# Two key heads and two chunks at once: pairing half-array matmuls in the attention and in the recurrent chain

## The chip, the cores and the metric

The kernel runs on one core of a Trainium2 chip. Its time is the device time of one launch in microseconds (us). Five engines run side by side, each through its own list of instructions in order: PE (TensorE, matmuls), DVE (VectorE), ACT (ScalarE), POOL (GpSimd) and SP (SyncE, which issues transfers here). PE multiplies a stationary operand, which it loads first, by a moving one that streams through.

## What is computed

A model block of 512 tokens by 1024 features in float32, and then two hybrid layers. Each hybrid layer runs three mixers on the same normed input (sliding-window attention, a gated recurrence, a retention), sums them under gates, and ends with a feed-forward part. The change touches two of the mixers. Cut to what matters:

```python
def sliding_window_attention(q, k, v, sinks):      # 8 query heads, 2 key heads of 64, blocks of 128
    s = einsum('bnqhgd,bnshd->bnhgqs', qb, kb) * 64 ** -0.5      # h: key head, g: its 4 query heads
    s = where(mask, s, -inf)                                     # a band of 128 keys back
    m = maximum(max(s), sink);  p = exp(s - m)
    p = p / (sum(p) + exp(sink - m))
    o = einsum('bnhgqs,bnshd->bnqhgd', p, vb)

def rwkv7_time_mix(...):                           # 8 heads of 64
    def step(S, (r, w, k, v, a, b)):
        Sa = S @ a
        S = S * w + outer(Sa, b) + outer(v, k)
        return S, S @ r                            # y: the outputs
```

## The kernel before, in words

Activations lie with features on the partitions, 512 tokens along the free axis. Dense products are done tile by tile (`dense`, `mac`): one M tile is 8 k tiles, each in three passes (lines 135 to 137) of a 128x128 weight against 512 tokens, 24 passes in all. The weight's two parts come from a cast on ACT (line 125, `whi`) and a subtraction on DVE (line 126, `wlo`); both have two buffers.

Dense tiles that nobody waits for yet stand in a queue, each with a cost of 5.2 or 5.6. The mixers call `pump(us)` between their own steps: it adds to a credit and starts as many queued tiles as the credit pays. `attention` pumps `pa` = 7.0 per block and key head, the chain `pc` = 2.5 per chunk. In the end a list scheduler at build time sets the order of instructions on every engine; the order is fixed before the launch.

**The chain** (`rwkv_chain`) goes through 8 chunks of 64 tokens in each layer. For chunk c, line 1001 adds what the state S[c] gives to `pr`, DVE copies it (line 1003), line 1012 multiplies it by the chunk's inverse, ACT copies the result into `UV` (line 1014), line 1020 makes the update of the state, POOL decays the old state (line 1026) and DVE adds the update in two halves (line 1030). `ahead(c+1)` (lines 970 and 976) prepares the next chunk apart from the state. The states stand in three buffers in turn (named srst, wd and wa in the trace). `outputs` makes a chunk's outputs: for each of 4 pairs of heads one product with the state (line 986, moving side 128 wide) and two with the values (line 989, 64 wide). The chunk's outputs go to 64 of the 128 PSUM partitions, the lower half for even chunks, the upper for odd ones, so they use one half of the array's columns. ACT copies them out (line 991).

**The attention** goes through 4 blocks of 128 queries. The key heads are in the two halves of the partitions: head 0 in rows 0 to 63 of `q` and `k`, head 1 in rows 64 to 127. For each block and each key head j in turn: scores of 4 query heads (line 1169, 64 rows of the array, 256 keys or, in the first block, 128), times scale and plus mask on DVE (line 1173), the row maximum (line 1175), exp on ACT (line 1184), division by the sum (line 1188), transposes on PE for each 128 keys (line 1192), a copy (line 1194), and the product with the values (line 1195: 64 columns of the array, moving side 512 wide) into the half of `po` that belongs to j. The score tiles `as` have two buffers.

A float32 product is done as two passes in the trace (so one instruction of the program stands as x2); a transpose and a float32r pass stand once.

## Time and profile before

| | |
|---|---|
| median of three timed runs | 2668.3 us (2667.89 to 2669.66) |
| profiled execution, first to last instruction (span) | 2666.0 us |
| what lies around the span, by the median | 2.3 us |
| PE busy | 2579.1 us, 97% of the span |
| DVE / ACT / POOL busy | 56% / 34% / 14% |
| one layer's chain (first layer) | about 860 to 941 us |
| one layer's attention (first layer) | about 1015 to 1125 us |

No time of its own is given for the profiled execution beside its span; the timed runs lie 1.9 to 3.7 us above the span. The second layer repeats chain and attention at about 1866 to 1941 us and 2020 to 2140 us. A row of the timeline begins with its start and the time from the first start to the last end of the merged instructions; ends of matmuls are modelled and overlap the next start, so what a group takes on PE is read from one row's start to the next row's start.

### The profile page before, as it was taken

Reading aid. Unit: us, or ns where it says so; the run is one execution under the profiler, and the core shown is the slowest. Engines: PE = TensorE matmul, PEld = TensorE weight load, DVE = VectorE, ACT = ScalarE, POOL = GpSimd, SP = SyncE. Lnnn points to the kernel's source line nnn. Section 1 sums busy time; section 2 is a strip of 40 time slices with the busy share of each in tenths; the row PEclk is TensorE's granted clock in tenths of the full one; section 3 lists DMA queues with packets and bytes.
Section 4 is the critical chain, followed back from the end, with each engine's and each line's share of the span. In section 5 each row is a group of like instructions: output and inputs, shape, how many; then the busy total and the mean of one; then the engine's idle time right before and its main releaser. Section 6 shows DMA issues by size and latency. Waiting matters only on the chain. (4 is left out here: it accounts for less than half of the span.)

```text
span 2666.0 us, 33302 instructions
## 1 busy us (share of the span) xinstructions
PE 2579.1 (97%) x13104; PEld 2052.8 (77%) x13104; DVE 1491.5 (56%) x2546; ACT 893.7 (34%) x1342; POOL 378.5 (14%) x277
## 2 busy tenths in 40 slices
PE   8989999999998999999999999998999999999999
PEld 6767888887776877677788887767877677788887
DVE  8775666336788455565443333788455565444322
ACT  4343444225332333522322222322333423332221
POOL 2111111013120001005311101120000004211100
PEclk9999999999999999999999999999999999999999
DMA  4132223334223143226422334223152226422332
GB/s 148 64 103 85 98 95 95 93 104 139 87 91 107 60 154 95 70 87 206 137 95 97 99 123 127 83 80 107 43 174 88 79 72 213 143 95 95 99 114 96
DMA packets 99502, 282.51 MB, mean 106 GB/s; under 512 B 13201, under 2 KB 14225, under 8 KB 99217
## 3 DMA queue, kind: packets, MB, share of 16 engines
q1 hardware_dynamic: 97616, 277.52, 31.8%
q10 hardware_dynamic: 1728, 2.87, 0.3%
q8 instruction: 103, 1.69, 0.3%
q14 instruction: 55, 0.44, 0.1%
HBM read 244.42 MB, written 31.72 MB: 104 GB/s over the span
## 5 line engine op out<-in xcount | busy, mean ns | idle before, releaser
L125 ACT CAST whi<-wraw 128x1024 fp32r<-128x1024 f32 (+1 forms) x400 | 414.6, 1037 | 1110.1 <-PE mm L136 735.1
L126 DVE TENSOR_TENSOR wlo<-wraw,whi 128x1024 fp32r<-128x1024 f32 (+1 forms) x400 | 491.9, 1230 | 246.6 <-ACT whi L125 237.1
L1352 POOL TENSOR_TENSOR fg<-fg,rb 128x512 f32<-128x512 f32 x44 | 78.3, 1780 | 396.1 <-ACT fg L1351 396.1
L135 PE MATMUL mm<-x0h,whi 128*128 128x512 f32 x286 | 116.2, 407 | 8.1 <-ACT x0h L165 8.1
L220 POOL TENSOR_TENSOR acc<-acc,sq 128x512 f32<-128x512 f32 x49 | 77.8, 1587 | 325.9 <-ACT sq L219 325.9
L137 PE MATMUL mm<-x0h,wlo 128*128 128x512 f32 x286 | 114.1, 399 | 6.0 <-DVE wlo L126 5.7
L135 PE MATMUL mm<-x2h,whi 128*128 128x512 f32 x286 | 114.3, 400 | 2.2 <-ACT x2h L165 2.2
L136 PE MATMUL mm<-x0l,whi 128*128 128x512 f32 x286 | 113.7, 397 | 1.2 <-DVE x0l L169 1.2
L136 PE MATMUL mm<-x2l,whi 128*128 128x512 f32 x286 | 114.6, 401 | 0.0
L136 PE MATMUL mm<-x5l,whi 128*128 128x512 f32 x286 | 112.9, 395 | 1.6 <-DVE x5l L169 1.6
L135 PE MATMUL mm<-x3h,whi 128*128 128x512 f32 x286 | 113.9, 398 | 0.0
L137 PE MATMUL mm<-x1h,wlo 128*128 128x512 f32 x286 | 113.7, 398 | 0.0
L136 PE MATMUL mm<-x3l,whi 128*128 128x512 f32 x286 | 113.1, 395 | 0.7 <-DVE x3l L169 0.7
L137 PE MATMUL mm<-x2h,wlo 128*128 128x512 f32 x286 | 113.7, 398 | 0.0
L136 PE MATMUL mm<-x1l,whi 128*128 128x512 f32 x286 | 113.3, 396 | 0.3 <-DVE x1l L169 0.3
L1354 DVE TENSOR_TENSOR fg<-fg,mm 128x512 f32<-128x512 f32 x44 | 30.3, 688 | 148.8 <-PE mm L137 148.8
L135 PE MATMUL mm<-x5h,whi 128*128 128x512 f32 x286 | 113.4, 397 | 0.0
L137 PE MATMUL mm<-x6h,wlo 128*128 128x512 f32 x286 | 113.3, 396 | 0.0
L135 PE MATMUL mm<-x6h,whi 128*128 128x512 f32 x286 | 113.3, 396 | 0.0
L135 PE MATMUL mm<-x7h,whi 128*128 128x512 f32 x286 | 113.2, 396 | 0.0
L137 PE MATMUL mm<-x7h,wlo 128*128 128x512 f32 x286 | 113.1, 396 | 0.0
L135 PE MATMUL mm<-x1h,whi 128*128 128x512 f32 x286 | 113.1, 395 | 0.0
(757 smaller groups left out, 6132.5 us busy)
## 6 DMA issues: line engine op xcount, KB each, us to landing
wraw<-in_w_in_dram SPq DMA_DIRECT2D x138, 512.0 KB, 3.5
wraw<-in_w_ffn_dram SPq DMA_DIRECT2D x88, 512.0 KB, 3.4
wraw<-in_w_up_dram SPq DMA_DIRECT2D x44, 512.0 KB, 3.3
wraw<-in_w_ffn_down_dram SPq DMA_DIRECT2D x32, 448.0 KB, 3.4
wraw<-in_w_out_dram SPq DMA_DIRECT2D x24, 512.0 KB, 3.5
gates<-gt SPq DMA_DIRECT2D x48, 256.0 KB, 2.1
cg<-gates SPq DMA_DIRECT2D x32, 256.0 KB, 3.8
gt<-xres SPq DMA_DIRECT2D x32, 256.0 KB, 3.3
```

What stands on the lines that cost most here:

```text
L125: nc.scalar.copy(hi[:, :n], raw[:, :n])
L126: nc.vector.tensor_tensor(lo[:, :n], raw[:, :n], hi[:, :n].bitcast(F32), ALU.subtract)
L135: self.nc.tensor.matmul(ps, hi[:, c], xh, start=first and k == 0, stop=False)
L136: self.nc.tensor.matmul(ps, hi[:, c], xl, start=False, stop=False)
L137: self.nc.tensor.matmul(ps, lo[:, c], xh, start=False, stop=last and k == n - 1)
L220: (eng or nc.gpsimd).tensor_tensor(acc, acc, s, ALU.add)
L1352: nc.gpsimd.tensor_tensor(g, g, rb, ALU.mult)
L1354: nc.vector.tensor_tensor(g, g, ps, ALU.mult)
```

## The change

In the chain, `outputs` is called only after every second chunk and makes the outputs of chunks c and c+1 together: for each step one product for the even chunk into partitions 0 to 63 and one for the odd chunk into 64 to 127, in turn. One ACT copy of 128 partitions takes the place of two of 64. `ahead(c + 1)` is written before the inverse's product rather than behind it. In the attention, the scores of both key heads are written in turn (row halves 0 and 1), both heads' softmaxes follow, then for each 128 keys both heads' transposes and copies, and then the two products with the values, one behind the other. `pump` is called once more for each 128 keys: 7.0 in the first block, 3.5 twice in the others, so that a layer's attention pays 84 of credit rather than 56. Otherwise the diff takes out comments and docstrings.

```diff
         def outputs(c, S, Y):
             py = self.tile(self.mm, [P, 512], "mm")
-            yo = slice(64 * (c % 2), 64 * (c % 2) + 64)
-            uv = UV[c % 2][:, c // 2]
             for p in range(4):
-                if S is not None:
-                    nc.tensor.matmul(py[yo, p * P:(p + 1) * P], AR[:, p, c, CH:], S[:, p], start=True, stop=False)
+                for e in range(2):
+                    if S[e] is not None:
+                        nc.tensor.matmul(py[64 * e:64 * e + 64, p * P:(p + 1) * P], AR[:, p, c + e, CH:], S[e][:, p],
+                                         start=True, stop=False)
                 for j in range(2):
                     h = 2 * p + j
-                    nc.tensor.matmul(py[yo, h * 64:h * 64 + 64], SC[:, h, c, CH:], uv[:, h * 64:h * 64 + 64],
-                                     start=S is None, stop=S is None or j == 1)
-            nc.scalar.copy(Y[yo], py[yo])
+                    for e in range(2):
+                        nc.tensor.matmul(py[64 * e:64 * e + 64, h * 64:h * 64 + 64], SC[:, h, c + e, CH:],
+                                         UV[e][:, c // 2, h * 64:h * 64 + 64], start=S[e] is None,
+                                         stop=S[e] is None or j == 1)
+            nc.scalar.copy(Y, py)
...
@@ -1001,10 +1004,11 @@
                         nc.tensor.matmul(pr[bh, p * P:(p + 1) * P], AR[:, p, c, 0:CH], S[c][:, p], start=False, stop=p == 3)
                 R = self.tmp(self.tb)
                 nc.vector.tensor_copy(R[bh], pr[bh])
-            if c:
-                if c % 2:
-                    Ys.append(self.tmp(self.tb))
-                outputs(c - 1, S[c - 1], Ys[-1])
+                if c < NCH - 1:
+                    nx = ahead(c + 1)
+            if c and c % 2 == 0:
+                Ys.append(self.tmp(self.tb))
+                outputs(c - 2, S[c - 2:c], Ys[-1])
             if c == NCH:
                 break
             pu = self.psum()
@@ -1013,7 +1017,6 @@
                                  start=True, stop=True)
             nc.scalar.copy(uv[bh], pu[bh])
             if c < NCH - 1:
-                nx = ahead(c + 1)
                 pS = self.psum()
                 for h in range(8):
                     o = slice(64 * (h % 2), 64 * (h % 2) + 64)
...
@@ -1157,22 +1160,23 @@
         ol = self.tile(op, [P, 4, T], "o1", F32R)
         for b in range(NW):
             k0 = 0 if b else P
-            nk = 256 - k0
-            po = self.psum()
-            for j in range(2):
-                o = slice(64 * j, 64 * j + 64)
-                s = self.tile(ap, [P, 4, 256], "as", bufs=2)
-                mx = self.small("am", 4)
-                for u in range(2):
-                    ps = self.psum()
-                    for i in range(2):
-                        nc.tensor.matmul(ps[:, i * 256 + k0:(i + 1) * 256], q[o, 2 * u + i, b * P:(b + 1) * P],
+            s = [self.tile(ap, [P, 4, 256], "as", bufs=2) for j in range(2)]
+            for u in range(2):
+                ps = [self.psum() for j in range(2)]
+                for i in range(2):
+                    for j in range(2):
+                        o = slice(64 * j, 64 * j + 64)
+                        nc.tensor.matmul(ps[j][:, i * 256 + k0:(i + 1) * 256], q[o, 2 * u + i, b * P:(b + 1) * P],
                                          k[o, (b - 1) * P + k0:(b + 1) * P], start=True, stop=True)
+                for j in range(2):
                     for i in range(2):
                         g = 2 * u + i
-                        nc.vector.scalar_tensor_tensor(s[:, g, k0:], ps[:, i * 256 + k0:(i + 1) * 256],
+                        nc.vector.scalar_tensor_tensor(s[j][:, g, k0:], ps[j][:, i * 256 + k0:(i + 1) * 256],
                                                        rq[:, b, g, j:j + 1], am[:, k0:], ALU.mult, ALU.add)
-                nc.vector.tensor_reduce(mx, s[:, :, k0:], AX.X, ALU.max)
+            for j in range(2):
+                mx = self.small("am", 4)
+                nc.vector.tensor_reduce(mx, s[j][:, :, k0:], AX.X, ALU.max)
                 nc.vector.tensor_tensor(mx, mx, sink[:, 4 * j:4 * j + 4], ALU.max)
                 nm = self.small("an", 4)
                 nc.vector.tensor_scalar(nm, mx, -1.0, None, ALU.mult)
@@ -1181,19 +1185,27 @@
                 nc.scalar.activation(es, es, AF.Exp)
                 dn = self.small("ad", 4)
                 for g in range(4):
-                    nc.scalar.activation(s[:, g, k0:], s[:, g, k0:], AF.Exp, bias=nm[:, g:g + 1], accum_out=dn[:, g:g + 1])
+                    nc.scalar.activation(s[j][:, g, k0:], s[j][:, g, k0:], AF.Exp, bias=nm[:, g:g + 1],
+                                         accum_out=dn[:, g:g + 1])
                 nc.vector.tensor_tensor(dn, dn, es, ALU.add)
                 nc.vector.reciprocal(dn, dn)
                 for g in range(4):
-                    nc.scalar.activation(s[:, g, k0:], s[:, g, k0:], AF.Copy, scale=dn[:, g:g + 1])
-                for z in range(k0 // P, 2):
+                    nc.scalar.activation(s[j][:, g, k0:], s[j][:, g, k0:], AF.Copy, scale=dn[:, g:g + 1])
+                self.pump(self.pa)
+            po = self.psum()
+            for z in range(k0 // P, 2):
+                pT = []
+                for j in range(2):
                     pt = self.psum()
                     for g in range(4):
-                        nc.tensor.transpose(pt[:, g * P:(g + 1) * P], s[:, g, z * P:(z + 1) * P], self.ident)
-                    pT = self.tmp(self.tb)
-                    nc.scalar.copy(pT, pt)
-                    nc.tensor.matmul(po[o], vt[:, b - 1 + z, o], pT, start=z == k0 // P, stop=z == 1)
-                self.pump(self.pa)
+                        nc.tensor.transpose(pt[:, g * P:(g + 1) * P], s[j][:, g, z * P:(z + 1) * P], self.ident)
+                    pT.append(self.tmp(self.tb))
+                    nc.scalar.copy(pT[j], pt)
+                for j in range(2):
+                    o = slice(64 * j, 64 * j + 64)
+                    nc.tensor.matmul(po[o], vt[:, b - 1 + z, o], pT[j], start=z == k0 // P, stop=z == 1)
+                self.pump(0.5 * self.pa if k0 == 0 else self.pa)
             c = slice(b * P, (b + 1) * P)
             p3 = po.rearrange("p (g t) -> p g t", g=4)
             nc.scalar.copy(oh[:, :, c], p3)
```

What it does to the order of PE, at three places of the first layer. In the rows, `mm` and `ps` are PSUM tiles, `AR`, `SC`, `UV` the chain's operands (UV of each parity), srst, wd and wa the states; a moving operand stands behind its arrow, the shape is that of the result.

**Outputs in the chain.** On PE, before, the end of chunk 2 (line 1001 for its state) and the first of the outputs of chunk 1:

```order
L1001 MATMUL ps_6783<-wd_6801,AR_5104 64x128 x4
L986 MATMUL mm_6846<-srst_6745,AR_5104 64x128
L989 MATMUL mm_6846<-UV_953_5110,SC_5103 64x64 x2
L986 MATMUL mm_6846<-srst_6745,AR_5104 64x128
L989 MATMUL mm_6846<-UV_953_5110,SC_5103 64x64 x2
```

Now, the first of the outputs of chunks 2 and 3 (line 991 is the former 989):

```order
L976 MATMUL ps_7013<-UV_953_5110,SC_5103 64x64 x8
L986 MATMUL mm_7023<-wd_6790,AR_5104 64x128
L986 MATMUL mm_7023<-wa_6893,AR_5104 64x128
L991 MATMUL mm_7023<-UV_952_5109,SC_5103 64x64
L991 MATMUL mm_7023<-UV_953_5110,SC_5103 64x64
L991 MATMUL mm_7023<-UV_952_5109,SC_5103 64x64
L991 MATMUL mm_7023<-UV_953_5110,SC_5103 64x64
```

Two chunks' products stand in turn, with the two states and the two `UV`, in one `mm` tile, where one chunk's stood alone.

**Scores and values in the attention.** On PE, before, where block 1's first key head is multiplied by the values and the first head of block 2 gets its scores:

```order
L136 MATMUL mm_8369<-x4l_5016,whi_8372 128x512
L137 MATMUL mm_8369<-x4h_5015,wlo_8373 128x512
L1195 MATMUL ps_8120<-t_8156,avt_7768 64x512
L1192 MATMUL ps_8159<-ident_80,as_8121 128x128 x4
L1169 MATMUL ps_8244<-ak_7672,aq_7775 128x256 x2
L1195 MATMUL ps_8120<-t_8164,avt_7768 64x512
L1169 MATMUL ps_8249<-ak_7672,aq_7775 128x256 x2
```

Now, the scores of block 1 (line 1170 is the former 1169), each `ps` tile one key head's:

```order
L137 MATMUL mm_8142<-x7h_5027,wlo_8146 128x512
L1170 MATMUL ps_8189<-ak_7664,aq_7767 128x256
L1170 MATMUL ps_8190<-ak_7664,aq_7767 128x256
L1170 MATMUL ps_8189<-ak_7664,aq_7767 128x256
L1170 MATMUL ps_8190<-ak_7664,aq_7767 128x256
L1170 MATMUL ps_8199<-ak_7664,aq_7767 128x256
L1170 MATMUL ps_8200<-ak_7664,aq_7767 128x256
L1170 MATMUL ps_8199<-ak_7664,aq_7767 128x256
L1170 MATMUL ps_8200<-ak_7664,aq_7767 128x256
L135 MATMUL mm_8228<-x0h_4999,whi_8231 128x512
```

Products of the two heads stand in turn where those of one head stood together.

**Products with the values.** On PE, now, in block 1 (lines 1202 and 1207 are the former 1192 and 1195):

```order
L137 MATMUL mm_8339<-x3h_5011,wlo_8343 128x512
L1202 MATMUL ps_8330<-ident_80,as_8188 128x128
L135 MATMUL mm_8339<-x4h_5015,whi_8342 128x512
L1202 MATMUL ps_8330<-ident_80,as_8188 128x128
L136 MATMUL mm_8339<-x4l_5016,whi_8342 128x512
L137 MATMUL mm_8339<-x4h_5015,wlo_8343 128x512
L1207 MATMUL ps_8322<-t_8328,avt_7760 64x512
L1207 MATMUL ps_8322<-t_8335,avt_7760 64x512
L135 MATMUL mm_8339<-x5h_5019,whi_8342 128x512
```

And in block 0:

```order
L135 MATMUL mm_8110<-x5h_5019,whi_8113 128x512
L1202 MATMUL ps_8101<-ident_80,as_7959 128x128
L1207 MATMUL ps_8093<-t_8099,avt_7760 64x512
L1202 MATMUL ps_8101<-ident_80,as_7959 128x128 x3
L136 MATMUL mm_8110<-x5l_5020,whi_8113 128x512
L137 MATMUL mm_8110<-x5h_5019,wlo_8114 128x512
L135 MATMUL mm_8110<-x6h_5023,whi_8113 128x512
L136 MATMUL mm_8110<-x6l_5024,whi_8113 128x512
L1207 MATMUL ps_8093<-t_8106,avt_7760 64x512
```

In block 1 the two heads' products are neighbours (there and for the second 128 keys, and so in block 2); in block 0 and block 3 something stands between them.

## Rows read from the trace of the kernel before

**Rows 1.** The page's first part: busy time, share of the span, instructions of each engine.
```profile
PE 2579.1 (97%) x13104; PEld 2052.8 (77%) x13104; DVE 1491.5 (56%) x2546; ACT 893.7 (34%) x1342; POOL 378.5 (14%) x277
```

**Rows 2.** Stretches, first layer's chain and attention: length, busy by engine, PE clock, DMA.
```profile
860.00:941.00 81.00, 78.10 (x761) 66.02 (x760) 40.58 (x102) 27.45 (x48) 6.30 (x6) 0.96 0.17 59
1015.00:1125.00 110.00, 109.77 (x455) 75.37 (x454) 64.30 (x127) 50.56 (x131) 11.01 (x8) 1.00 0.27 82
```

**Rows 3.** What PE waited for, same stretches: us in total, times, longest.
```profile
PE ps L976 <- DVE SC L934: 1.5, 2, 0.9
...
PE ps L1192 <- ACT as L1188: 0.2, 1, 0.2
```

**Rows 4.** Single lines of code: passes, ns min/median/max, first and last start, shapes.
```profile
L989 PE MATMUL mm<-UV,SC x256: 219/222/314, 869.5 to 1939.9; 128*64 128x64 f32 x128
...
L1169 PE MATMUL ps<-ak,aq x128: 272/376/480, 1009.1 to 2126.3; 64*128 64x256 f32 x96, 64*128 64x128 f32 x32
...
L1195 PE MATMUL ps<-t,avt x56: 592/618/644, 1024.8 to 2137.9; 128*64 128x512 f32 x56
...
L1026 POOL TENSOR_TENSOR wa<-wd,end x4: 1047/1050/1052, 878.7 to 1915.7; 128x512 f32<-128x512 f32 x4
```

**Rows 5.** Timeline of PE in the attention: start, us, engine, line, operands, passes.
```profile
1035.98 0.70 PE L1169 MATMUL ps<-ak,aq 64*128 64x256 f32 x2
1036.60 0.50 PE L135 MATMUL mm<-x2h,whi 128*128 128x512 f32 x1
...
1053.10 1.07 PE L1195 MATMUL ps<-t,avt 128*64 128x512 f32 x2
1054.10 1.13 PE L1169 MATMUL ps<-ak,aq 64*128 64x256 f32 x4
1055.16 0.50 PE L135 MATMUL mm<-x5h,whi 128*128 128x512 f32 x1
```

**Rows 6.** Timeline of PE in the chain, outputs of chunk 1.
```profile
882.71 0.38 PE L986 MATMUL mm<-srst,AR 128*64 128x128 f32 x2
882.93 0.40 PE L989 MATMUL mm<-UV,SC 128*64 128x64 f32 x4
883.16 0.38 PE L986 MATMUL mm<-srst,AR 128*64 128x128 f32 x2
```

**Rows 7.** Timeline of PE in the chain: one column half, then both in turn.
```profile
875.36 1.15 PE L976 MATMUL ps<-UV,SC 128*64 128x64 f32 x16
876.43 0.51 PE L137 MATMUL mm<-x1h,wlo 128*128 128x512 f32 x1
876.87 0.69 PE L1020 MATMUL ps<-UV,t 128*64 128x64 f32 x16
877.48 0.50 PE L135 MATMUL mm<-x2h,whi 128*128 128x512 f32 x1
877.82 0.39 PE L136 MATMUL mm<-x2l,whi 128*128 128x512 f32 x1
878.05 0.40 PE L137 MATMUL mm<-x2h,wlo 128*128 128x512 f32 x1
```

**Rows 8.** Timeline of PE ahead of the chain: row halves in turn.
```profile
701.75 2.49 PE L869 MATMUL ps<-AR,BK 64*128 64x128 f32 x32
704.17 0.50 PE L136 MATMUL mm<-x7l,whi 128*128 128x512 f32 x1
```

**Rows 9.** Timeline of DVE and ACT, one head's softmax in block 1.
```profile
1038.57 1.25 DVE L1173 SCALAR_TENSOR_TENSOR as<-ps,rq,amask 128x256 f32<-128x256 f32 x3
1039.86 1.22 DVE L1175 TENSOR_REDUCE am<-as 128x4 f32<-128x1024 f32 x1
...
1045.47 0.50 ACT L1184 ACTIVATE as<-as,an 128x256 f32<-128x256 f32 x1
...
1046.27 1.05 ACT L125 CAST whi<-wraw 128x1024 fp32r<-128x1024 f32 x1 [0.21 <-ACT as L1184]
1047.33 1.71 ACT L1188 ACTIVATE as<-as,ad 128x256 f32<-128x256 f32 x4
```

## The prediction

> **What bounds the kernel now.** The page's first part comes first: PE is busy 97% of the span, DVE 56%, ACT 34% [rows 1]. That is a mean over stages, so the next view is the busy time of the stretches that the change touches: in a layer's attention PE is busy 109.8 of 110 us, in its chain 78.1 of 81, at a clock that is full or nearly so (1.00 and 0.96 of the 2.4 GHz level) [rows 2]. The list of PE's waits says the same from the other side: in the attention PE waits 0.2 us, in the chain its longest entry is 1.5 us, at the start, for the inverse, which stays [rows 3]. The dense tiles fill every gap. So in these stretches a microsecond of PE work that goes is a microsecond of time, until something else is late; and the list scheduler places instructions so that they are just in time, which leaves little slack when PE gets faster.
>
> Last comes the timeline, for what a pass occupies on PE: the distance from start to start, since the modelled ends overlap.
>
> **What one half of the array costs, and two.** Line 1020 writes its 64 columns in turn to both halves: 16 passes take 0.61 us to the next start. Line 976 has the same shape and stays in one half: 16 passes take 1.07 us [rows 7]. Line 869 works in row halves in turn: 32 passes of 128 take 2.42 us [rows 8], where 0.11 us each in a row (below) would make 3.5 and two shape changes on top. So passes that lie in different halves and stand next to each other in PE's list run two at a time, in rows as in columns. What these rows have not: column halves with a moving side of 128 or 512 (lines 986 and 1195), row halves with 256 (line 1169).
>
> The Trainium skill speaks against the column half of this. "TensorE: Matmul & The Clock Gate", in its part on packing small matmuls, under "The mechanism", says that a weight load overlaps a running matmul only when its row group differs; two column halves share their row groups. By that rule line 1020 should have gone like line 976, so the trace does not bear it out for 64 columns; for 512 no run here shows it. I keep it as a rival.
>
> **The sum, term by term.**
>
> *Scores.* Two passes of 256 take 0.62 us to the next start, four take 1.06 [rows 5]: 0.22 a pass, and 0.18 for coming and going. A pass of 128 is half, 0.11, as line 986 confirms: two in 0.22 us [rows 6]. The trace has 96 and 32 passes [rows 4], a matmul being two. The pairs count only where the new order puts the heads next to each other. Per layer: block 0, four of eight matmuls, saves 2 x 0.22 = 0.44 us; blocks 1 and 2, all eight, 4 x 0.44 = 1.76 each; block 3, six of eight (two products with the values stand inside), 3 x 0.44 = 1.32. That is 5.3, for two layers **10.6 us**.
>
> *Products with the values.* 56 passes [rows 4], so 14 matmuls per layer, 7 possible pairs. Four are neighbours in the new order (blocks 1 and 2); in block 0 transposes and dense passes stand between, in block 3 a dense pass, and a full-array pass needs both halves. One matmul takes 1.00 us to the next start with its share of shape changes [rows 5], of which 2 x 0.44 = 0.88 is the work. 8 x 0.88 = **7.0 us**. Bounds: nothing, if 512 columns do not pair, and 14 x 1.00 = 14 us if the broken pairs cost nothing.
>
> *Outputs of the chain.* A quarter of one chunk is 0.45 us: 0.22 for line 986, 0.23 for two of line 989 [rows 6]; a chunk with a state is 1.81 us, chunk 0 without one 0.92. Chunks (2,3), (4,5) and (6,7) then take 1.81 together instead of 3.62; (0,1) takes the longer half. 3 x 1.81 + 0.92 = 6.35 per layer, less about 0.25 because dense passes split the last pair: 6.1, for both layers **12.2 us**. The copies (16 of them become 8) are on ACT, which has time.
>
> *Changes of tile shape.* A lone dense pass between two shapes takes 0.44 us instead of 0.23; so two changes cost 0.21 on the dense side. On the other side they cost 0.18 (the scores, above), or 0.07 (line 1020's 0.61 less eight pairs at a sixteenth of line 976's 1.07) [rows 5, 7]. Together 0.28 to 0.39 for two; I take 0.35, that is 0.175 for one. In the order of PE I count 292 changes before and 264 after: 28 x 0.175 = **4.9 us**. From 0 (if the paired forms hide them) to 28 x 0.21 = 6.
>
> Together 34.7 us less work on PE.
>
> **What the change adds.** *Softmax.* One head of a 256-key block took 0.42 us for each of four multiplies and 1.22 for the maximum on DVE, 0.50 for each exp and 1.71 for four scalings on ACT, and 10.5 us from the second multiply to the end of the scalings [rows 9], with foreign work in between. Now both heads' multiplies and both maxima, and in the order of ACT also the second head's exps, stand ahead of the first head's scalings: up to 1.7 + 1.2 + 2.0 = 4.9 us more, and 1.7 more to the second head's last. PE's cover from the scores to the first transpose is 48 dense passes in block 1, where it was 49: 11.0 us at 0.23 [rows 7]. My count of the new chain from the first score tile is 3.4 (eight multiplies) + 2.4 + 0.9 that I put for the small operations (no row here) + 2.0 + 1.05 for a cast in ACT's list [rows 9] + 2.0 + 0.9 for the first scalings and their hand-over = 12.6; PE gets there after 1.8 + 11.0 = 12.8. So it is close to nothing, and any delay shows: behind a transpose that waits stand dense passes, on which evictions and all further work depend. The paired scores also bring PE there 1.76 us earlier, while DVE begins about half of that earlier. I take that other half, 0.9 us, in six blocks of 256 keys, and 0.3 in two of 128: 6 us. Bounds: 0, and 4.9 + 1.7 = 6.6 in each of six and half in two, 46 us.
>
> The extra pumps cost nothing: five dense tiles that would have been flushed ahead of the retention run inside the attention, and the same number is left for the retention. The casts and subtractions for them move along on ACT and DVE, and their weight transfers on SP's queue, in the same order.
>
> *Chain.* `ahead` now runs while DVE copies `pr`, and needs the PSUM tile of that copy's neighbours; in even chunks lines 970 and 976 follow line 1001 at once. A state now lives until its pair's outputs, so the POOL decay that reuses its buffer (1.05 us [rows 4]) starts later; between it and its reader lie 16 passes of line 1012 like the 1.07 us of line 976, a copy, and line 1020's 0.61 [rows 7], so it is covered; without that cover it would cost its 1.05 in three chunks a layer. I take 1 us for all, from 0 to 6.
>
> **Forecast.** 34.7 - 7 = 27.7 us less. The sum stands against the profiled execution (span 2666.0, so 2638.3), and the timed runs lie 2.3 above the span at the median: 2668.3 - 27.7 = **2641 us**.
>
> **Rivals.** (1) *Column halves do not pair in the new places*, because the weight load of one half waits for the other's matmul. Then only scores and shape changes gain: 10.6 + 4.9 - 7 = 8.5, **2660 us**. For: no row shows a pair at 128 or 512. Against: [rows 7]. The rule of the Trainium skill that I weighed above would end here. (2) *The change doesn't do what it says*: no pair overlaps, 4.9 - 7, **2670 us**, no change. Against: [rows 7, 8]. (3) *Slower: the double softmax in front of the transposes.* With two `as` tiles, both taken by one block, nothing of the next block can start early; if its 6.6 us lie open in each block, 46 + 1 - 34.7 = 12 us more, **2680 us**. It decides from 40 us on, that is 5 us for each of eight blocks. For: DVE also carries the rotary work and a subtraction per tile there. Against: 48 to 68 dense passes stand in each block's gap. (4) *No wait at all*: 34.7 less, **2634 us**.
>
> **Chances.** Forecast with its own bounds, 2631 to 2656 (waits from 0 to about 20 us, the shape changes' bounds): 0.81, case 4 within it. Still better, because the split pairs gain too: 0.03. Case 1, or waits of 20 to 29 us: 0.08, still faster. Case 2: 0.04. Case 3: 0.04. Within 0.2% (5.3 us, about what a measurement of this kernel tells from no change) counts as the same. Faster 0.92, same 0.04, slower 0.04; the range is 2631 to 2656.
>
> **What would show it.** Right: lines 1169, 1195 (blocks 1 and 2) and 986/989 in pairs that start within some 10 ns; one pair of products with the values in about 1.0 us; a pair of chunks in about 1.8 us; no long entry of PE on the scalings of line 1188. Wrong: line 1195's second product starting 0.4 us or more behind the first (case 1), or PE waiting several us in each block for ACT (case 3), or idle ahead of line 976 in even chunks.

## The result and the profile after

The changed kernel took **2635.6 us** (median of 4 runs, 2630.5 to 2637.3) where the kernel before took 2668.1 beside it: a ratio of 0.9875, 95% interval 0.9862 to 0.9889. That is 32.5 us less. The forecast was 2641 in a range of 2631 to 2656. The profiled execution spans 2633.4 us, 32.6 less than before.

The page's first part of the changed kernel, the answer to [rows 1]:

```profile
PE 2543.2 (97%) x13104; PEld 2027.8 (77%) x13104; DVE 1492.5 (57%) x2546; ACT 885.8 (34%) x1334; POOL 380.0 (14%) x277
```

The number of matmul passes is the same; PE is busy 35.9 us less. The number of ACT instructions falls by the 8 copies of outputs that went.

**Pairs.** Three lines of the changed kernel, over the whole span (columns as in [rows 4]):

```profile
L1170 PE MATMUL ps<-ak,aq x128: 272/376/480, 1000.0 to 2080.8; 64*128 64x256 f32 x96, 64*128 64x128 f32 x32
...
L1207 PE MATMUL ps<-t,avt x56: 592/618/644, 1018.7 to 2109.6; 128*64 128x512 f32 x56
...
L991 PE MATMUL mm<-UV,SC x256: 219/222/270, 880.1 to 1916.0; 128*64 128x64 f32 x128
```

Minimum and median are those of [rows 4]: the duration of a pass doesn't show whether another ran beside it. That is seen from start to start, in the timeline of PE. The scores of block 1, and what follows them:

```profile
1028.65 2.00 PE L1170 MATMUL ps<-ak,aq 64*128 64x256 f32 x16
1030.57 0.50 PE L135 MATMUL mm<-x0h,whi 128*128 128x512 f32 x1
```

16 passes in 1.92 us to the next start, 0.12 each; four took 1.06 [rows 5], 0.265 each. The products with the values, first an unpaired one of block 0, then the two pairs of block 1:

```profile
1018.68 1.07 PE L1207 MATMUL ps<-t,avt 128*64 128x512 f32 x2
1019.68 0.55 PE L1202 MATMUL ps<-ident,as 128*128 128x128 f32 x3
...
1048.32 1.35 PE L1207 MATMUL ps<-t,avt 128*64 128x512 f32 x4
1049.60 0.50 PE L135 MATMUL mm<-x5h,whi 128*128 128x512 f32 x1
...
1053.33 1.56 PE L1207 MATMUL ps<-t,avt 128*64 128x512 f32 x4
1054.82 0.50 PE L137 MATMUL mm<-x0h,wlo 128*128 128x512 f32 x1
```

One product takes 1.00 us to the next start, two take 1.28 and 1.49 (the two pairs of block 2 take 1.17 and 1.23). They overlap, but not wholly: in the second pair of block 1 the four passes start 0.48, 0.01 and 0.48 us apart, so only the first head's second pass has another beside it. The outputs of chunks 2 and 3 (lines 986 and 991, the former 989):

```profile
896.88 0.32 PE L986 MATMUL mm<-wa,AR 128*64 128x128 f32 x1
896.93 0.22 PE L976 MATMUL ps<-UV,SC 128*64 128x64 f32 x1
896.99 0.28 PE L986 MATMUL mm<-wd,AR 128*64 128x128 f32 x1
897.04 0.27 PE L986 MATMUL mm<-wa,AR 128*64 128x128 f32 x1
897.10 0.27 PE L986 MATMUL mm<-wd,AR 128*64 128x128 f32 x1
897.15 0.40 PE L991 MATMUL mm<-UV,SC 128*64 128x64 f32 x7
897.38 0.28 PE L986 MATMUL mm<-wa,AR 128*64 128x128 f32 x1
...
897.84 0.28 PE L986 MATMUL mm<-wa,AR 128*64 128x128 f32 x1
...
898.89 1.14 PE L1016 MATMUL ps<-t,SC 64*64 64x64 f32 x16
```

The two states `wa` and `wd` come in turn, a quarter of both chunks takes 0.46 us (897.38 to 897.84), and both chunks are done 2.0 us after the first pass. One chunk alone took 1.81 before.

**Waits.** The attention of the changed kernel, what PE waited for (as in [rows 3]):

```profile
PE ps L1202 <- ACT as L1193: 2.9, 2, 2.0
PE ps L1246 <- DVE t L1072: 0.5, 1, 0.5
PE ps L1170 <- DVE o L1212: 0.3, 1, 0.3
...
```

Line 1193 is the scaling of the softmax (1188 before), line 1202 the transposes. The longer of the two is in block 1. Here is its chain on DVE and ACT, and then its end on PE:

```profile
1029.61 1.23 DVE L126 TENSOR_TENSOR wlo<-wraw,whi 128x1024 fp32r<-128x1024 f32 x1 [0.16 <-ACT whi L125]
1030.75 3.22 DVE L1175 SCALAR_TENSOR_TENSOR as<-ps,rq,amask 128x256 f32<-128x256 f32 x8
1033.89 2.33 DVE L1179 TENSOR_REDUCE am<-as 128x4 f32<-128x1024 f32 x2
...
1036.53 0.51 ACT L1188 ACTIVATE as<-as,an 128x256 f32<-128x256 f32 x1 [6.96 <-DVE an L1182]
...
1043.18 0.91 ACT L1193 ACTIVATE as<-as,ad 128x256 f32<-128x256 f32 x2 [1.45 <-DVE ad L1191]
...
1043.74 0.33 PE L1202 MATMUL ps<-ident,as 128*128 128x128 f32 x1 [1.95 <-ACT as L1193]
```

From PE's first score (1028.65) to its first transpose pass it is 15.1 us: 13.1 for the scores and the 48 dense passes behind them, the rest is the wait.

**Where the time went.** The table sums, for the first layer, the time from each PE pass to the next one's start, by line (numbers of the kernel before); a wait counts with the pass ahead of it. "Chain" is here the stretch from the last pass of line 869 to the attention's first pass (line 1127, now 1130), and "attention" the stretch from there to the retention's first pass (line 1268, now 1280). Both begin and end in dense passes, so they are longer than the stretches of [rows 2].

| us, first layer | before | after | change | forecast |
|---|---|---|---|---|
| outputs, lines 986 and 989 | 15.1 | 8.1 | -6.9 | -6.1 |
| lines 970, 976, 1012, 1020 | 30.5 | 24.9 | -5.6 | 0 |
| other lines of the mixer in the chain | 19.3 | 18.3 | -1.0 | shapes |
| dense passes in the chain (467) | 120.9 | 123.6 | +2.8 | shapes |
| scores | 16.0 | 8.9 | -7.1 | -5.3 |
| products with the values | 14.0 | 11.2 | -2.9 | -3.5 |
| transposes of the scores | 6.6 | 6.0 | -0.6 | shapes |
| dense passes in the attention (497) | 118.7 | 122.6 | +3.9 | waits, +3 |

The chain takes 185.7 us before and 174.9 after, the attention 162.6 and 155.8; in the second layer 186.7 and 175.2, 162.9 and 156.5. The four differences are 35.5 us; the rest of the span, in which no line is changed, was 2.9 us longer. It varies like that from run to run (the stretch ahead of the first chain was between 783.7 and 786.0 us), so the smaller verdicts below go by the length of the stretch.

Two of the rows hold waits of the kernel before that are gone. What PE waited for from 860 to 950, before, has these entries behind those of the chain's start:

```profile
...
PE mm L135 <- ACT BK L165: 0.7, 1, 0.7
PE ps L1012 <- DVE rst L187: 0.5, 1, 0.5
```

The first stands behind line 1047 ("other lines"), the second behind one chunk's outputs (first row). The changed kernel has two waits in that stretch, 0.4 and 0.6 us, both behind dense passes. So 0.7 of the 1.0 and 0.5 of the 6.9 are waits, and 1.0 of the 2.8 too.

**A gain that wasn't forecast.** The table's second row is won at the start of the chain alone: from chunk 2 on, line 976 takes 1.0 us a chunk in both kernels. PE's timeline there before:

```profile
861.17 0.65 PE L976 MATMUL ps<-UV,SC 128*64 128x64 f32 x8 [0.87 <-DVE SC L934]
862.50 0.68 PE L976 MATMUL ps<-UV,SC 128*64 128x64 f32 x8 [0.67 <-DVE SC L934]
863.96 1.97 PE L1012 MATMUL ps<-t,SC 64*64 64x64 f32 x16 [0.79 <-DVE t L1003]
...
869.51 1.68 PE L989 MATMUL mm<-UV,SC 128*64 128x64 f32 x16
871.12 0.51 PE L135 MATMUL mm<-x0h,whi 128*128 128x512 f32 x1
```

and after:

```profile
862.02 0.40 PE L136 MATMUL mm<-x0l,whi 128*128 128x512 f32 x1
862.82 0.65 PE L976 MATMUL ps<-UV,SC 128*64 128x64 f32 x8 [0.40 <-DVE SC L934]
...
865.17 0.50 PE L137 MATMUL mm<-x0h,wlo 128*128 128x512 f32 x1
...
866.06 1.14 PE L1016 MATMUL ps<-t,SC 64*64 64x64 f32 x16
867.13 0.50 PE L137 MATMUL mm<-x1h,wlo 128*128 128x512 f32 x1
```

Before, no dense pass stood between the inverse's products (line 929, from 857.5) and the end of chunk 0's outputs. PE waited three times, 2.3 us in all, and 16 passes of line 1012 took 1.97 us instead of 1.14, because the clock had fallen. The stretch of 12 us from 860, before and after (columns as in [rows 2]; the third number from the end is the clock):

```profile
860.00:872.00 12.00, 9.68 (x92) 8.43 (x91) 3.92 (x7) 2.34 (x4) 1.05 (x1) 0.72 0.17 63
```

```profile
860.00:872.00 12.00, 11.60 (x197) 9.26 (x191) 5.41 (x8) 3.01 (x6) 1.05 (x1) 1.00 0.20 67
```

The clock was 0.72 on the mean there, part of the time at the 1.2 GHz level, and is 1.00 of 2.4 GHz now: dense passes fill the gaps from 861.7 on. Ahead of the chain nothing differs: from the first pass of line 917, behind the 5.1 us wait for the inverse, 12 us have a clock of 0.87 in both kernels, and line 970 begins 12.5 us behind that pass in both. In the second layer the clock was 0.57 in the 12 us from 1866 and is 1.00 in the same part now. The gain thus has two parts that make up nearly all of it: of the waits 1.9 us went, and the clock's share is an estimate of 3.4 us (12 us at 0.72), 0.6 of it in chunk 0's outputs. In every trace of a kernel with the chain's pairs the clock stays at 1.00 from the chain's first line 970 to its end, and in those without them (the kernel before, e2 and e3) it falls in both layers. Whether the waits brought it down or the small passes around them, no run shows.

### The profile page after: what moved, and what is told of

The parts are those of the page before. It is cut to its first block, busy times and chain, and to the rows that moved or that the text cites. A ratio compares the mean times of both kernels' runs of the same rounds, so it can differ in the third digit from the quotient of the medians.

```text
span 2633.4 us, 33268 instructions
## 1 busy us (share of the span) xinstructions
PE 2543.2 (97%) x13104; PEld 2027.8 (77%) x13104; DVE 1492.5 (57%) x2546; ACT 885.8 (34%) x1334; POOL 380.0 (14%) x277
## 5 line engine op out<-in xcount | busy, mean ns | idle before, releaser
L1364 POOL TENSOR_TENSOR fg<-fg,rb 128x512 f32<-128x512 f32 x44 | 78.3, 1780 | 396.1 <-ACT fg L1363 396.1
L135 PE MATMUL mm<-x4h,whi 128*128 128x512 f32 x286 | 113.5, 397 | 0.0
L136 PE MATMUL mm<-x7l,whi 128*128 128x512 f32 x286 | 113.4, 396 | 0.0
```

Of the source, the lines that this page charges most:

```text
L135: self.nc.tensor.matmul(ps, hi[:, c], xh, start=first and k == 0, stop=False)
L136: self.nc.tensor.matmul(ps, hi[:, c], xl, start=False, stop=False)
L1364: nc.gpsimd.tensor_tensor(g, g, rb, ALU.mult)
```

## The experiments

Unless said otherwise an edit is made to the changed kernel; ratios are to the kernel before, on the same chip.

### The two halves of the change by themselves

e1 is the kernel before with the change to the chain alone, e2 with the change to the attention alone.

> The chain's part of the change alone, the attention as before. Theory (each part's gain stays in its own stretch, since TensorE is the bound in both): from the chain's last scores to the attention's first product the two traces differ by 10.7 us in the first layer and 11.5 in the second, of which about 1 belongs to what follows; so 19 to 21 us less than before, 2648 us. Rival (the parts help or hinder each other, for instance because dense tiles change places between them): 12 or less, or 26 or more.

> The attention's part of the change alone, the chain as before. Theory: 6.8 and 6.3 us less in the two layers by the two traces, 13 us, 2655 us, and with the run of the chain alone it adds up to the 32.5 us of the whole. Rival: the sum of the two is over 4 us away from the whole.

e1: 2647.3 us, ratio 0.9917 (0.9904 to 0.9929). e2: 2654.9 us, 0.9946 (0.9934 to 0.9959). Both as expected, and the parts add: spans shorter by 20.4 and 12.8 us make 33.2, the whole change 32.6. The chain's part is the larger one.

### The chain: the pairs, or the new place of `ahead`

e3 is the kernel before with `ahead` moved up, outputs still one chunk at a time; e4 has outputs for two chunks, and `ahead` in its old place.

The edit of e3:

```diff
+                if c < NCH - 1:
+                    nx = ahead(c + 1)
...
-                nx = ahead(c + 1)
```

> Only the preparation of the next chunk (lines 970 and 976) is written ahead of the inverse's product; outputs stay one chunk at a time, attention as before. Theory A (the chain's gain is the pairing of outputs): 0 to 2 us less, 2667 us. Theory B (the trace after shows lines 970, 976 and 1012 cheaper by 1.8, 2.7 and 0.8 us per layer, and that comes from the new place alone): 5 to 10 us less, 2660 us.

> Outputs of two chunks in pairs, but the preparation of the next chunk in its old place; attention as before. Theory A (pairing is all of the chain's gain): as the chain's part alone, 20 us less, 2648 us. Theory B (the new place gives its own share): 12 to 15 us less, 2654 us, and together with the run that moves only the preparation it adds up to the chain's part.

e3: 2660.1 us, 0.9964 (0.9952 to 0.9977). e4: 2650.4 us, 0.9926 (0.9914 to 0.9938). e3 came out as its theory B had it, e4 nearer to its theory A; but e3's seven runs lie between 2654.7 and 2667.1 us, at mean clocks of 0.990 to 0.984, so its median says little. By the length of the two chains e3 gains 5.2 us, e4 20.4 and e1 22.4: the two together are 3.2 over e1, so part of the gain can be had by either. Look at the 12 us from 860 again, e3 first and then e4:

```profile
860.00:872.00 12.00, 9.68 (x117) 8.61 (x117) 4.69 (x8) 2.35 (x5) 1.05 (x1) 0.86 0.18 67
```

```profile
860.00:872.00 12.00, 11.60 (x205) 9.27 (x199) 5.75 (x9) 2.81 (x5) 0.85 (x1) 1.00 0.19 67
```

With the pairs alone the start of the chain is filled and at full clock; with `ahead` alone PE is as idle as before, at a clock a little higher. The four lines of the table's second row, 30.5 us before and 24.9 now, take 28.1 in e3 and 25.4 in e4. So the unforecast gain comes with the pairs. In the code chunk 0's outputs and the dense tiles take their PSUM tiles from one pool, `mm`; before, the first dense pass behind line 929 stood after chunk 0's outputs in PE's order, and with the pairs those outputs come later. That this is why the dense passes can move up fits both runs, but no run changed the pool, so it is argued and not shown.

### The attention: which of the pairs are worth something

e5 lets a head's product with the values follow its own transposes, as before the change; e6 has all scores of one head ahead of the other's.

The edit of e6, its beginning:

```diff
-            for u in range(2):
-                ps = [self.psum() for j in range(2)]
-                for i in range(2):
-                    for j in range(2):
-                        o = slice(64 * j, 64 * j + 64)
+            ps = [[self.psum() for j in range(2)] for u in range(2)]
+            for j in range(2):
+                o = slice(64 * j, 64 * j + 64)
+                for u in range(2):
+                    for i in range(2):
...
```

> The changed kernel, but each head's product with the values directly behind its own transposes and copy, so that the two are no neighbours. Theory (the pairs save what the trace after shows, 14.0 - 11.2 = 2.85 us per layer): 5.7 us more than the changed kernel, about 2641 us. Rival (the columns' pairing at 512 is not what saved it, the shape changes around it are): under 2 us more.

> The changed kernel, but a block's scores are written head by head, so that neighbours lie in one row half; softmax, transposes and values as changed. Theory: 5.3 us of overlap per layer go, one border per block still pairs (0.4), so 8 to 10 us more than the changed kernel, about 2644 us; shape changes stay. Rival (the paired scores only bring TensorE sooner to the transposes, where it waits for ACT): 3 us more or less, with the waits on the scalings shorter than the 6.1 us they are.

e5: 2635.9 us, 0.9876 (0.9863 to 0.9888). The products take 12.7 us a layer instead of 11.2, and the attention 157.6 and 157.7 instead of 155.8 and 156.5: 3 us for two layers, too little for the median to tell and less than the 5.7 expected. But the list scheduler, which has the last word on PE's order, put two of the four pairs of a layer together all the same:

```profile
1053.11 1.56 PE L1205 MATMUL ps<-t,avt 128*64 128x512 f32 x4
...
1088.00 1.30 PE L1205 MATMUL ps<-t,avt 128*64 128x512 f32 x4
```

So e5 takes apart half of the pairs. The four pairs of the changed kernel take 5.2 us a layer where eight products alone take 8.0: pairing the values is worth 2.8 us a layer, all of that row's gain and 5.7 us for both, not 7.

e6: 2633.8 us, 0.9871 (0.9858 to 0.9884), no loss. Yet its scores do take longer. Block 1:

```profile
1026.90 2.96 PE L1170 MATMUL ps<-ak,aq 64*128 64x256 f32 x16
1029.80 0.50 PE L135 MATMUL mm<-x0h,whi 128*128 128x512 f32 x1
```

2.90 us to the next start instead of 1.92, and 11.3 a layer instead of 8.9. But PE's wait for the scalings is 2.2 us in that attention instead of 2.9, and the attention only 0.9 and 0.3 us longer. The expectation of 8 to 10 us more was wrong: what the pairing of the scores gains is given back in front of the transposes and in the dense passes, as the rival had it. The larger part of the scores' gain, from 16.0 to 11.3 us a layer, is kept in e6. About half of that are passes which still overlap where the two heads meet (16 at 0.22, with 0.18 for coming and going, would be 3.7 us, not 2.90). The rest isn't the pairing: the passes of a layer's scores stand in 6 groups in e6 and in the changed kernel, while before they stood in 20, with other work behind every few [rows 5]. At 0.19 us for each coming and going, worked out from those 20 groups, 14 groups fewer are 2.7 us; so overlap is worth 4.7 us a layer in the changed kernel, and 2.3 of that are left in e6.

### The added pumps

The changed kernel calls `pump` behind the products with the values too. e7 leaves that out (credit of 56 us in an attention instead of 84), e8 doubles it (112).

```diff
-                self.pump(0.5 * self.pa if k0 == 0 else self.pa)
+                self.pump(self.pa if k0 == 0 else 2 * self.pa)
```

(the line of e8; e7 has only the line with the minus)

> The changed kernel without the added pumps, so the attention draws as many dense tiles as before and the rest is flushed ahead of the retention. In the order of TensorE 45, 57, 53, 52 dense passes stand between a block's scores and its first transpose, where the changed kernel has 45, 48, 52, 68. Theory (a wait follows from the cover of its own block): block 1's wait of 2 us shrinks, block 3 gets one; all in all within 3 us of the changed kernel. Rival (the added pumps are what keeps the double softmax hidden): 6 us or more above it.

> The changed kernel with the added pumps doubled: 45, 72, 68, 72 dense passes of cover per block. Theory: TensorE's waits for the scalings (6.1 us in all) go, 4 to 6 us less than the changed kernel, about 2631 us. Rival (what the attention draws is missing later, in the retention, where its waits on DVE and ACT grow): no change or more.

e7: 2626.8 us, 0.9848 (0.9835 to 0.986): by the ratios 7 us less than the changed kernel, where at most 3 were expected. "The extra pumps cost nothing" was wrong. As many dense passes run by the attention's end (497), but 57 instead of 48 stand ahead of block 1's first transpose, and PE's waits there are, in the same stretch:

```profile
PE ps L1170 <- DVE o L1211: 1.1, 3, 0.4
...
```

The wait on the scalings is gone, PE changes between full and half tiles 22 times in the attention instead of 28, and it takes 153.0 and 152.7 us, 2.8 and 3.8 less, which is the 7 us. The scores pair less well there (11.9 us a layer, 1.1 of it waits), so this isn't yet the best order.

e8: 2679.5 us, ratio 1.0042 (1.003 to 1.0054), slower than before the change: the theory was wrong, the rival had it. Its attention holds 617 dense passes instead of 497, and the retention behind it lacks them. What PE waits for from 1130 to 1800, e8:

```profile
PE ps L1320 <- DVE t L653: 15.2, 4, 5.4
```

In the changed kernel that entry (from 1110 to 1780, the same part) is 1.8 us, four times at most 0.8. And the clock falls with it, e8:

```profile
1160.00:1190.00 30.00, 19.79 (x158) 16.78 (x158) 20.87 (x63) 4.11 (x6) 1.27 (x2) 0.89 0.26 88
1190.00:1220.00 30.00, 23.43 (x97) 19.18 (x94) 12.99 (x30) 4.46 (x6) 7.50 (x5) 0.66 0.17 52
```

Here is a mechanism that turns the sign of the whole change: the dense passes are a store, and with 120 fewer of them the retention can't hide its norms (line 653). The changed kernel leaves the retention as many as before (2540 from its start to the next chain), as the prediction said; what it costs there is the place inside the attention.

### More or fewer, or elsewhere

e10 keeps the sum of the pumps and moves all of it into the softmax.

```diff
-                self.pump(self.pa)
+                self.pump(1.5 * self.pa)
...
-                self.pump(0.5 * self.pa if k0 == 0 else self.pa)
```

> The changed kernel with the same sum of pumps in the attention (84 us of credit), but all of it in the softmax (1.5 times as much after each head), none between the products with the values. In PE's order 92, 94, 74 and 91 dense passes then stand between the scores and the first transpose of a block, where it was 45, 48, 52 and 68. Theory (the added pumps cost time by their place: they split the transposes and the products with the values, and they leave too few dense passes ahead of the transposes): no wait on the scalings is left and the attention takes about 153 us a layer, as without the added pumps: 2625 to 2629 us. Rival (dense tiles drawn into the attention cost time wherever they stand): 2634 us or more.

2625.2 us, 0.9837 (0.9823 to 0.985): as the theory has it. No wait on the scalings, 20 changes between full and half tiles, 151.4 and 151.0 us of attention. So it is the place of the added pumps that costs some 10 us (by the ratios and by the two stretches), not their sum.

### The line that still stands alone

In the changed kernel line 976 still writes one column half at a time. e9 makes `ahead` for two chunks at once, in both halves in turn.

```diff
...
+                for e in range(2):
+                    nc.tensor.matmul(pr[rows(c + e), h * 64:h * 64 + 64], SC[:, h, c + e, 0:CH],
+                                     UV[e][:, c // 2, h * 64:h * 64 + 64],
+                                     start=h == 0, stop=c + e == 0 and h == 7)
...
```

> The changed kernel, with `ahead` made for two chunks at once: the transposes of both, and line 976 with the products of the two chunks in turn, one in each column half. Theory (what stands alone in one column half costs double): line 976 has 128 passes a layer and takes 7.7 us there; at the 0.61 us for 16 passes of line 1020 that is 4.9, so 2.8 us less a layer, and some 1 us more for shape changes that go, since a pair of chunks is entered once: 6 to 8 us in all, 2628 to 2630 us. Rival (line 976 already overlaps with the products that stand next to it, and two chunks' worth at once makes the recurrence wait): within 3 us of 2635.6.

2628.0 us, 0.9845 (0.9831 to 0.9858). Line 976, now 979, at the chain's start:

```profile
864.32 0.69 PE L979 MATMUL ps<-UV,SC 128*64 128x64 f32 x16
864.94 0.50 PE L135 MATMUL mm<-x1h,whi 128*128 128x512 f32 x1
```

16 passes in 0.62 us to the next start, where one half took 1.07 [rows 7]. The line takes 5.2 us a layer instead of 7.7, line 1001 takes 4.7 instead of 6.4, and the chain 170.5 and 170.8 us instead of 174.9 and 175.2, 8.8 us less. The attention behind it is 1.9 and 1.4 us longer than in the changed kernel, its longest wait on the scalings 2.4 us instead of 2.2. Behind that wait the clock falls, which it doesn't do in the changed kernel's attention (1.00 in the same 10 us):

```profile
1036.00:1046.00 10.00, 7.62 (x30) 5.46 (x30) 4.94 (x10) 6.68 (x17) 0.43 (x1) 0.83 0.52 147
```

It is 0.83 in the second layer too. 10 us at 0.83 cost 1.7 us by estimate, which is about the difference.

### Both together

e11 is e9 without the added pumps, e12 is e9 with them moved as in e10.

> `ahead` for two chunks at once, and the added pumps left out. The two stand in different stretches (chain and attention), so by the theory both gains are there in full: 7 to 9 us for the pumps and 6 to 8 us for `ahead`, 2619 to 2623 us. Rival (line 976 gains nothing): 2627 us, as without the added pumps alone.

> `ahead` for two chunks at once, and the added pumps moved into the softmax. By stretches: the chain as with `ahead` for two (170.6 us a layer, 4.4 less than the changed kernel), the attention as with the moved pumps (151.2 us, 5.0 less), 18.8 us for two layers: 2615 to 2619 us. Rival (the two hinder each other, since the credit that is left over moves the dense tiles of both stretches): 2621 us or more.

e11: 2617.8 us (2616.9 to 2619.5), ratio 0.9809 (0.9796 to 0.9822), 1.2 us below what was expected. e12: 2614.4 us (2608.8 to 2621.8), ratio 0.9788 (0.9774 to 0.9801), 0.6 us below what was expected; its spread reaches over e11's, so which of the two is better is open. Both beat the changed kernel, by the ratios by 18 and 23 us.

e12's profiled execution is the slowest of its five (2621.8 us). Its attention takes 150.8 and 151.6 us, as in e10, but its chain 173.2 us in both layers where e9's took 170.5 and 170.8. Up to 1010 us the order of PE is the same in e9 and e12. Here are the 12 us from 850, e9 first and then e12:

```profile
850.00:862.00 12.00, 12.00 (x277) 10.26 (x277) 4.92 (x6) 3.91 (x7) 0.00 (x0) 0.92 0.25 83
```

```profile
850.00:862.00 12.00, 12.00 (x156) 9.26 (x155) 2.24 (x3) 2.83 (x5) 0.00 (x0) 0.65 0.20 68
```

The same passes, with no wait in this stretch in either, had a clock of 0.92 once and of 0.65 once (in e11 0.73 in the first layer, where its chain took 173.2 us too). In e12 it was 0.99 from 855 to 858, while the 32x32 passes of line 917 ran, and 0.50 from 858.5 to 861.5 behind them, with PE busy throughout. So these 3 us or so a layer differ from execution to execution and don't come from e12's edit.

## Why the prediction was right, and where it wasn't

**Pairs in the new places: right.** Row halves at 256 columns, column halves at 64, 128 and 512 run beside each other, at 512 in part. Rivals 1 and 2 are out. By the prediction's own signs the values are the weak place: their second products start 0.17 to 0.48 us behind the first and not some 10 ns, and one of a layer's four pairs lies beyond the 0.4 us that it gave as the sign of case 1. The Trainium skill's rule that a weight load overlaps a running matmul only when its row group differs ("TensorE: Matmul & The Clock Gate", "The mechanism") isn't borne out: two chunks' outputs in column halves take 2.0 us where one took 1.81.

**Outputs, 12.2 us: right.** 6.9 us a layer were measured where 6.1 were forecast. Some 0.6 of them belong to the clock: chunk 0's outputs took 1.61 us to the next start (869.51 to 871.12, above), and the prediction's 0.92 would be theirs at full clock. 0.5 is the wait that went. That leaves 5.8: a pair of chunks takes 2.0 us, not 1.81.

**Waits: right in sum, wrong in place.** 6 us of waiting in front of the transposes were forecast as 0.9 in each large block; measured are 6.1 in both layers, in the first 1.95 us in block 1 and 0.93 in block 2, and 2.2 more in other places of the attention, 7.7 us over the kernel before in all. The count of the chain's work was close: multiplies 3.2 for 3.4, maxima 2.3 for 2.4, exps and a cast 5.1 for 5.05. What it lacked is foreign work in DVE's queue: the multiplies began 2.1 us behind the first score pass, behind a subtraction of the weights, and the scalings had to wait 1.45 us for a small DVE operation that stood behind rotary work. Rival 3 had the right mechanism, but no block came near its 5 us. (Block 0's gap holds 45 dense passes, fewer than the 48 to 68 it names; PE had no wait there.)

**"It stays": the step that failed.** Of the waits at the start of the chain the prediction says that they are for the inverse and stay. They didn't: 2.3 us of waits became 0.4, and a clock of 0.72 became 1.00. With the two smaller waits that went, waits and clock give 13 us in the two chains, where the prediction had put 1 us of loss. The row with 0.96 [rows 2] held the sign of it: a mean over 81 us hid 12 us at 0.72.

**Shape changes, 4.9 us: mis-sized.** Without waits and clock the other small passes of the mixers got some 2.3 us a layer cheaper, and the scores 2.7 by their 14 fewer groups; but the dense passes got dearer, by 1.9 us in the chain and 1.5 in the attention (means of the two layers). That leaves a gain of some 3 us for two layers. The count of 28 fewer changes was right but hid that they fall from 53 to 30 in a layer's attention and rise from 56 to 65 in its chain.

**Scores and values, 10.6 and 7.0 us.** The scores gained 7.1 us a layer, 7.4 without the 0.3 of waits that stand in them now: 4.7 by overlap, where 5.3 were forecast, and the 2.7 of the last paragraph. Of the 2.4 us that only the order in pairs gives, the attention keeps 0.9 and 0.3 (e6). The values gained 2.8 instead of 3.5, since two products overlap by a quarter to four tenths and not by half.

**The extra pumps: wrong.** They were put at nothing; left out they give 7 us (e7), elsewhere 10 (e10).

So it was luck that the forecast missed by only 5 us. Each of its terms came out a little worse: for two layers the shapes by 1.9 us, the waits of the attention by 1.7, the values by 1.3, the scores by 1.2 and the outputs by 0.6. The 13 us of waits and clock in the chains, where 1 us of loss was forecast, outweighed that and the 2.9 us by which the rest of the span was longer.

## What to carry to other kernels

Look for passes that write or read half of the tensor engine and stand alone in PE's list: putting the other half's passes next to them nearly halves them (at 512 columns they gain a quarter to four tenths), but the gain is kept only where something else doesn't then come late, so check the work that the pairs wait for (both heads' softmax) and give it enough independent passes ahead of its reader. Where a queue of filler work feeds several stages, ask of each filler pass which gap it is taken from; doubling a pump turned a gain of 32 us into a loss of 11. A stretch whose clock is below 1.00 on the mean is to be cut into finer stretches before it is called fixed: the slow part may be a few us that an edit elsewhere can fill.

## What the runs showed of the hardware

- Two column halves with a moving side of 512 overlap only in part: 1.17 to 1.49 us for two products that take 1.00 each alone. Row halves with 256 overlap nearly wholly (1.92 us for 16 passes); their second pass starts 0.007 us behind the first.
- A fall of the clock can cost more than the waits ahead of it: behind three waits of 2.3 us in all, line 1012's 16 passes took 1.97 us instead of 1.14, in 12 us with a mean clock of 0.72 (some 3.4 us lost by estimate); behind a wait of 2.4 us the clock was 0.83 over 10 us (e9), while behind one of 2.0 us it stayed at 1.00 (the changed kernel). With PE busy for 19.8 of 30 us the next 30 us had a clock of 0.66 (e8).
- It can also fall with no wait, and in one execution but not in another: with PE busy for all of 12 us the mean clock was 0.92 in e9 and 0.65 in e12, with the same passes in the same order; in e12 it fell from 0.99 to 0.50 behind the 32x32 passes of line 917.
- Two matmuls of different lines overlap as well if their halves differ: in the rows of chunks 2 and 3 the next quarter's first pass of line 986 starts while line 991's passes of the quarter before still run (897.38).
